# The second product of the attention scores over 128 rows instead of 64

## The chip, the cores and the metric

The kernel runs on one core of a Trainium2 chip. Its time is the device time of one execution in microseconds (us). The kernel before was timed three times: 2665.77, 2670.35 and 2674.51 us, median 2670.35 us. All arithmetic that the program sees is 32 bit; matrix products run on TensorE (PE), elementwise work on VectorE (DVE), ScalarE (ACT) and GpSimd (POOL), and most transfers are issued from SyncE's queue (SP).

## The reference, cut to what matters

The reference is one step of a four-layer decoder trunk of width 1024, for 512 tokens of a prompt and 8 single tokens of a sample group. Layer 1 mixes the tokens by dilated window attention, in three groups of 16 heads of 64 channels. The three groups have dilations 1, 4 and 16, and their outputs are merged by their softmax denominators. For the prompt, each group does this:

```
logits = einsum('brnqhd,brnkhd->brnhqk', qb, kb) * (Dh ** -0.5) + bias
logits = where(valid, logits, -1e30)
p = exp(logits - max(logits));  s = sum(p)
o = einsum('brnhqk,brnkhd->brnqhd', p, vb) / s;  lse = max + log(s)
```

The scores of one head thus contract over 64 channels. Before them stands `qkv = h @ w_qkv` (1024 by 9216), behind them `y @ w_o`.

## The kernel before, in words

Every 32-bit value that goes into a product is split into a rounded part hi and a rest lo (`copy` into a tile of the rounded type, then `tensor_sub`), and a product is the sum of hi by hi, lo by hi and hi by lo. `mm3` (lines 390 to 395) does this for the large products: three matmuls of 128 rows, on weights `wh`, `wh`, `wl` and moving operands `mh`, `ml`, `mh`. Tokens come in two chunks, CA (264 columns) and CB (256 columns).

The attention (`attn`, line 659) goes over eight pairs of heads. While pair `hp` is attended to (`attend`), the products of queries, keys and values of pair `hp + 1` (`qkv`) are put between its steps; behind the last pair it is the output's product (`attn_out`). A planner gives each engine one fixed order of instructions from this program and gives each tile a place in SBUF; a tile that takes the place of an earlier one waits for the last reader there. SyncE's queue works in order, so a transfer that waits for its place holds up those behind it.

For each pair and group, `qkv` leaves two tiles of 128 rows for the scores. In `qs`, a head's 64 rows of hi and its 64 rows of lo stand one above the other; in `ks` the keys' hi stands twice. One matmul over 128 rows gives hi by hi and lo by hi (line 927). The third part, hi of the queries by lo of the keys, is a second matmul over 64 rows: `qs[own]` with `kl[own]`, where `kl` is `[128, 512]`, with head 0 in rows 0 to 63 and head 1 in rows 64 to 127 (line 928). `kl` has three places in rotation.

`attn_units` makes the scores of two blocks of 128 queries: these matmuls, and then, for each block, a DVE pass that adds the bias and finds the minimum (L932) and an ACT exponential (L933). It is called eight times for a pair of heads: `scores_g0` four times and `scores_g12` four times. The biases come from DRAM by SyncE's queue (L939, L953), into a tile with three places. Later steps take the weights of the merge (`attn_weights`, POOL copies at L971 and L972), scale the exponentials (L1012, ACT), turn them (L1018, PE), split them (L1022, L1023) and multiply them by the values (L1038 to L1040). The exponentials lie in the place of `x`, which rests in DRAM meanwhile (`self.pr`); the outputs go to `y`.

The sample group's attention (`attn_sample`) goes along in steps: a transposed tile `st` that is sent to DRAM and read back spread out as `qt`, cache tiles `skv`, products on POOL (L1081, L1111) and sums on DVE (L1086, L1115) into a tile `part`.

The ring `w` of five places (`self.tp`, tag `w`) is used by the norms at a sublayer's start and end, and not in the middle of the attention. POOL has the additions `x + t` (L239) and some of the norms' sums (L222, L333) at the attention's start.

Of the kernel before, what the change touches and what calls it, by code (L numbers as in the profile page):

```python
# [36 lines left out]
# By the sublayer (0 to 7), and where a chunk is named by that too: which engine takes a share, and what goes first.  # L37
# [16 lines left out]
class Net:  # L54
# [19 lines left out]
    @contextmanager  # L74
    def phase(self, extra=0, start=0):
        """Working memory of a sublayer; extra: more tiles for weights beside the four that all share."""
        with ExitStack() as e:
            P = lambda name: e.enter_context(self.tc.tile_pool(name=self.n(name), bufs=1))
            lp = self.lp = P("lp")
            self.wx, self.wextra, self.wcount = (P("wx") if extra else None), extra, start  # L80
            yield lp
            self.wx = None
# [11 lines left out]
    # ---------------------------------------------------------------- set-up  # L94
# [17 lines left out]
    def load(self):  # L112
        """The tokens and the vectors by channel; the tokens are staged where the hidden units of chunk B will lie."""
# [33 lines left out]
    def load_tokens(self, t):  # L147
        """Block t of the tokens, channels on partitions."""
# [9 lines left out]
    def stir(self, n):  # L158
        """Products that nobody reads: TensorE's clock rises only while it works."""
        ps = self.psum(128, 128)  # L160
        for _ in range(n):
            self.nc.tensor.matmul(ps, self.ones, self.ones, start=True, stop=True)
# [4 lines left out]
    # ---------------------------------------------------------------- norms  # L167
    def rstat(self, acc, c, dim=D, eps=None):
        """acc [128, w]: per-partition sums of squares; returns 1/sqrt(sum/dim + eps) on all partitions (PSUM)."""
# [20 lines left out]
    def mean(self, acc, c):  # L190
        """The sum over the channels, on all partitions (PSUM)."""
# [5 lines left out]
    def post(self, gain):  # L197
        """The norm at a sublayer's end; gain(b): its factors (by channel) for block b of the output."""
        return {"gain": gain, "at": self.at}

    def post_block(self, post, ps, b, c, part=None, bias=None, scale=1.0, near_end=False):
        """One finished block of a sublayer's output: kept in y, its squares summed."""
# [21 lines left out]
    def post_end(self, post, c, next_row):  # L224
        """x += y * gain * r for chunk c, then the next sublayer's moving operand: by blocks; chunk B's is deferred."""
# [27 lines left out]
    def flush(self):  # L253
        """What the sublayer before left to be put behind the first products of this one."""
        self.run(self.deferred)

    def in_products(self, ww, c, rr, evac, fill=None):
        """Four products of chunk c, which evac(pg) takes up; at a sublayer's start the norms' work goes between."""
# [30 lines left out]
    def step_hooks(self):  # L289
        """Side work goes on a little: generators that load first and compute some steps later."""  # L290
# [4 lines left out]
    def out_order(self, goes_on=False):  # L295
        """The order of the last products' pairs of blocks: chunk A whole, then chunk B, and there first those
        whose weights' places the next sublayer's weights take."""
# [3 lines left out]
    def out_step(self, post, i, next_row):  # L301
        """After the i-th of the last products."""
# [19 lines left out]
    def pre_sums(self, c, at):  # L322
        """Per-partition sums of x's squares for the next norm, chunk c."""
# [11 lines left out]
    def pre_r(self, c):  # L335
        """1/rms of x for chunk c, in SBUF on all partitions."""
# [6 lines left out]
    # ---------------------------------------------------------------- weights  # L343
# [3 lines left out]
    def weights(self, ap, wide=False):  # L347
        """ap: up to 1024 rows by 128 columns in DRAM (wide: 128 rows by up to 1024 columns);
        returns the parts hi, lo as [128, blocks, 128]."""
# [19 lines left out]
    def behind(self, instructions):  # L369
        """What is traced within is issued after these, each on its own engine."""  # L370
# [5 lines left out]
    def ffn_in_weights(self, layer, jp):  # L376
        """Of the feed-forward's jp-th pair of hidden blocks: gate and up of each; perhaps loaded ahead."""
# [4 lines left out]
    def load_ahead(self, n):  # L382
        """The next n weights of the feed-forward that follows."""
# [13 lines left out]
    # ---------------------------------------------------------------- feed-forward  # L397
    def place(self, c, dtype):
        """Room for a third of chunk c's hidden units, in parts hi and lo; other sublayers use it in between."""
# [63 lines left out]
    # ---------------------------------------------------------------- pooling mixer  # L463
    def pool_bands_load(self):
        """What a token takes from the tokens before it, a band for each window, and from the sample group's history."""
# [3 lines left out]
    def pool(self, layer, j, post_row, next_row, begin=None):  # L469
        """The windows' means less the token are products of the normed tokens with bands of constants."""  # L470
# [49 lines left out]
    def pool_history(self, j):  # L520
        """What the windows take from the sample group's earlier inputs."""
# [13 lines left out]
    def pool_tokens(self, st, c):  # L535
        """The two blocks of tokens of chunk c, normed (but for the gain by channel), tokens on partitions."""
# [32 lines left out]
        if c == CB:  # L569
            # the last tokens, with the gains, are the prompt's new state  # L570
# [6 lines left out]
    def pool_sample(self, st):  # L577
        """The sample group's tokens: channels on partitions all along."""
# [22 lines left out]
    def pool_means(self, st, c, ahead=()):  # L601
        """Means less the token for chunk c: the moving operand of the pooling's product."""
# [25 lines left out]
    def pool_products(self, st, c, ahead=()):  # L628
        """ahead: the blocks before which a weight of the feed-forward is prepared."""
# [28 lines left out]
    # ---------------------------------------------------------------- attention mixer  # L658
    def attn(self, post_row, next_row):
# [4 lines left out]
        with self.phase() as self.ws:  # L664
            self.r = {}
            self.scr = [self.dram.tile([72, 128], F32, name=f"scr{i}") for i in range(8)]
            # x rests in DRAM meanwhile; its place holds the exponentials, y's the outputs
# [3 lines left out]
            self.wnext = None  # L671
            heads = [dict() for _ in range(9)]
# [18 lines left out]
    def attn_out(self):  # L691
        """The output's product of the first seven pairs of heads, as far as it hides behind the last pair."""
# [20 lines left out]
    def attn_out_end(self, post_row, next_row):  # L713
        """The rest: the last pair of heads, and the products that are left to hide the norm of chunk A."""
# [24 lines left out]
    def bias_setup(self):  # L739
        nc, I = self.nc, self.I  # L740
        # relative biases (negated, and 1e30 outside the window) as one row per head
# [31 lines left out]
        # the rows laid out for every query of a block, so that a head's biases load as one tile  # L773
# [16 lines left out]
    def qkv_weights(self, i):  # L790
        """Weights of the i-th product: for each pair of heads, queries and keys of each group, then values."""
# [4 lines left out]
    def qkv(self, hp, out):  # L796
        """Queries, keys (feature-major) and values (token-major) of a pair of heads, in parts hi and lo."""
# [7 lines left out]
        for gqs in ([(0, 1, 2)] if hp == 0 else []) + [(gq,) for gq in range(0 if hp else 3, 9)]:  # L805
# [21 lines left out]
            for gq, t in zip(gqs, ts):  # L827
                g, q = QKV_ORDER[gq]
                # of each head: the queries' parts hi and lo, one above the other, and for both the keys' part hi
# [6 lines left out]
                elif q == 1:  # L836
                    ks = ws.tile([128, 2, SEQ], F32R, tag="ks", name=self.n("ks"), bufs=3)
                    kl = ws.tile([128, SEQ], F32R, tag="kl", name=self.n("kl"), bufs=3)
                    for h, own, oth in HALVES:
                        nc.scalar.copy(ks[own, h], t[own])  # L840
                        nc.scalar.copy(ks[oth, h], t[own])
                        nc.vector.tensor_sub(kl[own], t[own], ks[own, h].bitcast(F32))
# [4 lines left out]
    def qkv_part(self, what, c, ps, t, sq9):  # L847
        """A finished product of chunk c, scaled, in the order of the group's residue classes."""
# [21 lines left out]
    def token_major(self, hp, g, q, t, out):  # L870
        """Keys and values with the tokens on partitions, for the caches and as the values' weights."""
# [19 lines left out]
    def attend(self, hp, kv):  # L891
        """Attention of a pair of heads; yields where other products can be put between."""
# [26 lines left out]
    def attn_units(self, h, units, bias, stat, lay, p):  # L919
        """Scores of two blocks of queries of head h: units = [(block, first key column, products)]."""  # L920
        nc, ws = self.nc, self.ws
        own = HALVES[h][1]
# [544 lines left out]
```

## Time and profile before

| what | value |
|---|---|
| median of three runs | 2670.35 us |
| the profiled execution's span, first to last instruction | 2664.7 us |
| PE busy / weight loads busy | 95% / 92% of the span |
| DVE / ACT / POOL busy | 66% / 50% / 19% |
| mean granted TensorE clock | 0.974 |
| the attention, from the first product to the last pair's end | about 455 to 1130 us |

The profiled execution has no time of its own beside its span; the span is 5.65 us below the median of the runs. A busy PE is not a PE at its peak: a matmul's record lasts from its start until its result has left, and the next one starts before that. So the distance from the start of one matmul to the start of the next tells what it costs. Weight loads have rows of their own (PEld).

### The profile page before, as it was taken

How to read it: one execution, taken by the hardware profiler on the slowest of the kernel's cores; microseconds unless marked ns; L12 is line 12 of the kernel's file. 1: busy time of each engine (PE TensorE's matmuls, PEld its weight loads, DVE VectorE, ACT ScalarE, POOL GpSimd, SP SyncE). 2: the span in 40 equal slices, each digit the busy share in tenths (PEclk: the TensorE clock that was granted, in tenths of full speed). 3: DMA queues.
4: the chain of work that ended last, by engine and by line, in shares of the span. 5: the costliest groups of instructions: out<-in, count | busy, mean ns of one | idle time of the engine just before them, and what ended most of it. 6: DMA issues, size and time to landing. Idle time of an engine off the chain costs nothing.

```text
span 2664.7 us, 50514 instructions
## 1 busy us (share of the span) xinstructions
PE 2539.0 (95%) x20200; PEld 2459.1 (92%) x20200; DVE 1762.4 (66%) x3063; ACT 1329.1 (50%) x2484; POOL 502.0 (19%) x661
## 2 busy tenths in 40 slices
PE   7999999999999999989999997679999998999998
PEld 7899999999999999889999985569999998999998
DVE  5746565677777777577474589987647456756564
ACT  6534344556655556455342373466534246644342
POOL 3100003123233322320000047622000004200002
PEclk8999999999999999999999998789999999999999
DMA  4575553444443443356464430023746452555451
GB/s 142 164 215 167 150 151 107 139 126 120 128 131 114 134 137 114 115 152 178 143 184 121 124 96 1 16 82 93 203 142 183 119 151 65 143 166 175 143 158 57
DMA packets 653432, 349.76 MB, mean 131 GB/s; under 512 B 14865, under 2 KB 649730, under 8 KB 652910
## 3 DMA queue, kind: packets, MB, share of 16 engines
q1 hardware_dynamic: 648996, 338.10, 43.9%
q0 software_dynamic: 1232, 6.06, 0.8%
q8 instruction: 159, 2.61, 0.4%
q10 hardware_dynamic: 2969, 2.37, 0.4%
q14 instruction: 76, 0.61, 0.1%
HBM read 331.87 MB, written 20.68 MB: 132 GB/s over the span
## 4 chain that ended last, share of the span: by engine, by line
PE 41%; DVE 7%; ACT 1%; POOL 1%; issue 1%; DMA 0%; DVEq 0%; ACTq 0%; POOLq 0%; SPq 0%
PE mm L393 13%; PE mm L394 13%; PE mm L395 13%; DVE y L1269 4%; DVE wl L365 1%; POOL acc L222 0%; PE mm L186 0%; POOL x L239 0%; ACT wh L364 0%; DVE y L1267 0%; DVE y L1274 0%; DVE ml L319 0%; DMA raw<-in_w_ffn_in_dram 0%; PE mm L615 0%; ACT mh L318 0%
## 5 line engine op out<-in xcount | busy, mean ns | idle before, releaser
L393 PE MATMUL mm<-mh,wh 128*128 128x264 f32 (+1 forms) x4544 | 1316.5, 291 | 34.2 <-DVE u L1179 19.9
L394 PE MATMUL mm<-ml,wh 128*128 128x264 f32 (+1 forms) x4544 | 1295.0, 285 | 5.6 <-DVE ml L319 5.4
L395 PE MATMUL mm<-mh,wl 128*128 128x264 f32 (+1 forms) x4544 | 1290.5, 284 | 0.7 <-DVE wl L365 0.7
L393 PEld LDWEIGHTS mm<-mh,wh 128*128 128x128 f32 x4544 | 865.0, 191 | 47.5 <-DVE u L1179 21.8
L364 ACT CAST wh<-raw 128x1024 fp32r<-128x1024 f32 (+1 forms) x557 | 574.0, 1036 | 661.8 <-PE mm L394 406.1
L394 PEld LDWEIGHTS mm<-ml,wh 128*128 128x128 f32 x4544 | 867.8, 191 | 11.5 <-DVE ml L319 8.7
L365 DVE TENSOR_TENSOR wl<-raw,wh 128x1024 fp32r<-128x1024 f32 (+1 forms) x557 | 691.8, 1246 | 279.9 <-ACT wh L364 277.0
L395 PEld LDWEIGHTS mm<-mh,wl 128*128 128x128 f32 x4544 | 865.8, 191 | 1.2 <-DVE wl L365 1.1
L393 PE MATMUL mm<-h,wh 128*128 128x264 f32 (+1 forms) x1408 | 398.5, 283 | 1.6 <-DVE pr L1154 1.6
L394 PE MATMUL mm<-h,wh 128*128 128x264 f32 (+1 forms) x1408 | 397.6, 282 | 0.8 <-DVE h L422 0.8
L395 PE MATMUL mm<-h,wl 128*128 128x264 f32 (+1 forms) x1408 | 397.9, 283 | 0.0
L222 POOL TENSOR_TENSOR acc<-acc,sq 128x264 f32<-128x264 f32 (+1 forms) x90 | 78.5, 872 | 1387.4 <-ACT sq L221 1384.1
L393 PEld LDWEIGHTS mm<-h,wh 128*128 128x128 f32 x1408 | 265.2, 188 | 2.6 <-issue 2.2
L394 PEld LDWEIGHTS mm<-h,wh 128*128 128x128 f32 x1408 | 265.2, 188 | 1.2 <-DVE h L422 1.0
L395 PEld LDWEIGHTS mm<-h,wl 128*128 128x128 f32 x1408 | 265.1, 188 | 0.1
L1269 DVE SCALAR_TENSOR_TENSOR y<-conv_u,vec,y 128x512 f32<-128x512 f32 (+1 forms) x136 | 131.4, 1001 | 0.0
L419 DVE TENSOR_TENSOR u<-mm,r 128x264 f32<-128x264 f32 (+1 forms) x176 | 74.8, 425 | 84.9 <-PE mm L395 84.8
L239 POOL TENSOR_TENSOR x<-x,xt 128x264 f32<-128x264 f32 (+1 forms) x111 | 97.7, 904 | 93.0 <-DVE xt L234 91.4
L1263 POOL TENSOR_TENSOR tapa<-tapa,tapp 128x512 f32<-128x512 f32 (+1 forms) x76 | 104.8, 1379 | 18.3 <-DVE y L1274 12.5
L456 DVE TENSOR_TENSOR y<-mm,y 128x264 f32<-128x264 f32 x64 | 24.0, 429 | 124.5 <-PE mm L395 124.5
L933 ACT ACTIVATE x<-x,own 128x256 f32<-128x256 f32 (+1 forms) x128 | 62.4, 489 | 87.8 <-DVE own L932 87.7
L417 DVE TENSOR_TENSOR g<-mm,r 128x264 f32<-128x264 f32 (+1 forms) x176 | 74.8, 425 | 42.5 <-PE mm L395 38.9
(221 smaller groups left out, 2704.0 us busy)
## 6 DMA issues: line engine op xcount, KB each, us to landing
raw<-in_w_ffn_in_dram SPq DMA_DIRECT2D x352, 512.0 KB
raw<-in_w_qkv_dram SPq DMA_DIRECT2D x72, 512.0 KB
raw<-in_w_ffn_out_dram SPq DMA_DIRECT2D x64, 512.0 KB
skv<-in_cache_swa_g_dram SPq DMA_DIRECT2D x32, 512.0 KB
raw<-in_w_ffn_out_dram SPq DMA_DIRECT2D x32, 384.0 KB
out_dram<-tm SPq DMA_DIRECT2D x32, 256.0 KB
raw<-in_conv_w_in_dram SPq DMA_DIRECT2D x16, 512.0 KB
bias<-bias_full SPq DMA_DIRECT2D x32, 128.0 KB
```

Source lines behind the costliest of these rows:

```text
L222: (eng or nc.vector).tensor_add(post[c], post[c], sq)
L239: self.added = nc.gpsimd.tensor_add(xb, xb, t)
L364: whi = nc.scalar.copy(wh, raw)
L365: self.parted = whi, nc.vector.tensor_sub(wl, raw, wh.bitcast(F32))
L393: nc.tensor.matmul(ps, wh[:, k, :], mh, start=first, stop=False)
L394: nc.tensor.matmul(ps, wh[:, k, :], ml, start=False, stop=False)
L395: nc.tensor.matmul(ps, wl[:, k, :], mh, start=False, stop=last)
L417: nc.vector.tensor_mul(g, pg[2 * i], rr[c])
L419: nc.vector.tensor_mul(u, pg[2 * i + 1], rr[c])
L933: nc.scalar.activation(pc, pc, AF.Exp, scale=-1.0, bias=stat[:, lay, 0, c:c + 1], accum_out=stat[:, lay, 1, c:c + 1])
L1263: nc.gpsimd.tensor_add(a2, ap, pr)
L1269: nc.vector.scalar_tensor_tensor(yb, win(ub, t), wd[:, b, t:t + 1], yb, op0=ALU.mult, op1=ALU.add)
```

## The change

`kl` becomes `[128, 2, 512]`, one half for each head. Head `h` has its own 64 rows of lo in `kl[own, h]`; the other 64 rows of that half are zero. The three tiles are made once, at the attention's start, and POOL sets their zero halves. The second matmul then takes all 128 rows: the queries' rows of lo meet the zeros. To make room, small tiles go elsewhere: the biases and `st` into the ring `w`, `qt` into the part of `y` that the last pair of heads will fill, and two of the three blocks of `part` into columns of `self.pr` that no block of queries uses. Comments and docstrings are gone.

```diff
             self.pending, self.late = [], []
             self.wnext = None
+            self.kl = [self.ws.tile([128, 2, SEQ], F32R, name=f"kl{i}") for i in range(3)]
+            for kl in self.kl:
+                for h, own, oth in HALVES:
+                    nc.gpsimd.memset(kl[oth, h].bitcast(F32), 0.0)
...
-                    kl = ws.tile([128, SEQ], F32R, tag="kl", name=self.n("kl"), bufs=3)
+                    kl = self.kl[(hp * 3 + g) % 3]
                     for h, own, oth in HALVES:
                         nc.scalar.copy(ks[own, h], t[own])
                         nc.scalar.copy(ks[oth, h], t[own])
-                        nc.vector.tensor_sub(kl[own], t[own], ks[own, h].bitcast(F32))
+                        nc.vector.tensor_sub(kl[own, h], t[own], ks[own, h].bitcast(F32))
...
-        own = HALVES[h][1]
...
                 nc.tensor.matmul(out, qs[:, h, qc], ks[:, h, kc], start=True, stop=False)
-                nc.tensor.matmul(out, qs[own, h, qc], kl[own, kc], start=False, stop=True)
+                nc.tensor.matmul(out, qs[:, h, qc], kl[:, h, kc], start=False, stop=True)
...
-            bias = ws.tile([128, 256], F32, tag="bias", name=self.n("bias"), bufs=3)
+            bias = self.tp.tile([128, 264], F32, tag="w", name=self.n("bias"), bufs=5)[:, :256]
...
-        st = ws.tile([72, 128], F32, tag="st72", name=self.n("st72"), bufs=1)
+        st = self.tp.tile([128, 264], F32, tag="w", name=self.n("st72"), bufs=5)[:72, :128]
...
-        qt = ws.tile([128, 3, 128], F32, tag="sqt", name=self.n("sqt"), bufs=1)
+        qt = self.y[:, 7, NS:NS + 384].rearrange("p (g f) -> p g f", g=3)
...
-        part = ws.tile([128, 3, 128], F32, tag="spart", name=self.n("spart"), bufs=1)
+        part = [ws.tile([128, 128], F32, tag="spart", name=self.n("spart"), bufs=1)] + [self.pr[0][h][:, 0, 0:128] for h in range(2)]
```

## Rows read from the trace of the kernel before

**Rows 1.** Busy time by stretch: us, then PE, PEld, DVE, ACT, POOL, clock, DMA.
```profile
674.00:701.00 27.00, 27.00 (x170) 22.88 (x168) 18.26 (x48) 14.58 (x40) 15.21 (x27) 1.00 0.38 110
701.00:748.00 47.00, 47.00 (x418) 46.82 (x419) 36.20 (x66) 28.19 (x56) 8.02 (x14) 1.00 0.46 133
...
1065.00:1091.00 26.00, 26.00 (x150) 21.67 (x149) 10.08 (x32) 11.39 (x37) 12.67 (x27) 0.95 0.33 94
```

**Rows 2.** Groups by line, 460 to 1130 us: count, busy us, mean ns, idle before.
```profile
L928 PE MATMUL mm<-kl,qs 64*128 64x128 f32 x192 | 65.0, 339 | 0.0
```

**Rows 3.** PE in order of time, a call of `scores_g12`: start, duration, what.
```profile
687.96 0.22 PE L927 MATMUL mm<-ks,qs 128*128 128x128 f32 x1
688.11 0.33 PE L928 MATMUL mm<-kl,qs 64*128 64x128 f32 x1
688.37 0.33 PE L927 MATMUL mm<-ks,qs 128*128 128x128 f32 x1
...
689.90 0.39 PE L393 MATMUL mm<-mh,wh 128*128 128x256 f32 x1
690.12 0.28 PE L394 MATMUL mm<-ml,wh 128*128 128x256 f32 x1
```

**Rows 4.** PE, first and last rows of two calls of `scores_g0`.
```profile
674.27 0.22 PE L927 MATMUL mm<-ks,qs 128*128 128x128 f32 x1
...
675.53 0.28 PE L394 MATMUL mm<-ml,wh 128*128 128x264 f32 x1
...
676.87 0.27 PE L927 MATMUL mm<-ks,qs 128*128 128x256 f32 x1
...
678.23 0.28 PE L394 MATMUL mm<-ml,wh 128*128 128x256 f32 x1
```

**Rows 5.** Matmuls and weight loads in order of time, around a first score product.
```profile
673.19 0.28 PE L393 MATMUL mm<-mh,wh 128*128 128x264 f32 x1
673.19 0.19 PEld L394 LDWEIGHTS mm<-ml,wh 128*128 128x128 f32 x1
673.31 0.29 PE L394 MATMUL mm<-ml,wh 128*128 128x264 f32 x1
...
674.42 0.18 PEld L928 LDWEIGHTS mm<-kl,qs 64*128 64x128 f32 x1
674.43 0.32 PE L928 MATMUL mm<-kl,qs 64*128 64x128 f32 x1
```

**Rows 6.** PE, matmuls of 128 columns elsewhere in the attention.
```profile
640.65 0.22 PE L1038 MATMUL mm<-th,vh 128*64 128x128 f32 x1
640.71 0.22 PE L1039 MATMUL mm<-tl,vh 128*64 128x128 f32 x1
...
643.61 0.60 PE L1018 MATMUL mm<-ident,x 128*128 128x128 f32 x4
643.97 0.37 PE L393 MATMUL mm<-mh,wh 128*128 128x256 f32 x1
```

**Rows 7.** DVE, ACT and PE behind the last scores of a pair.
```profile
701.18 0.42 DVE L932 CUSTOM_DVE_ANT_0 x<-mm,bias 128x256 f32<-128x256 f32 x1 [1.16 <-PE mm L928]
...
707.42 4.00 ACT L1012 ACTIVATE x<-x,ca 128x256 f32<-128x256 f32 x10
...
711.33 0.60 PE L1018 MATMUL mm<-ident,x 128*128 128x128 f32 x4
```

**Rows 8.** POOL: a memset (group by line), and its order around the attention's start.
```profile
L1165 POOL MEMSET conv_u<- 128x240 f32 x1 | 0.3, 288 | 0.0
...
456.80 2.14 POOL L239 TENSOR_TENSOR x<-x,xt 128x264 f32<-128x264 f32 x3
...
462.61 0.75 POOL L333 TENSOR_TENSOR acc<-acc,sq 128x264 f32<-128x264 f32 x1 [1.88 <-DVE acc L333]
```

**Rows 9.** Waits of SyncE's queue, 500 to 1100 us: total us, times, longest.
```profile
SPq L953 <- DVE own L932: 43.0, 10, 6.3
SPq L354 <- DVE own L932: 35.9, 7, 5.3
```

More of the change, by code (lines that the diff above doesn't have):

```diff
@@ L951, in scores_g12 @@
         for h in range(2):
-            bias = ws.tile([128, 256], F32, tag="bias", name=self.n("bias"), bufs=3)
+            bias = self.tp.tile([128, 264], F32, tag="w", name=self.n("bias"), bufs=5)[:, :256]
             nc.sync.dma_start(bias, self.bias_full[2 * hp + h, :, 256:512])
@@ L1114, in attn_sample @@
         for (g, o, n), vt in zip(SLOTS, vts):
-            nc.vector.tensor_reduce(part[:, g, :], vt.rearrange("p s f -> p f s"), axis=AX.X, op=ALU.add)
-        nc.vector.tensor_add(part[:, 0, :], part[:, 0, :], part[:, 1, :])
-        nc.vector.tensor_add(part[:, 0, :], part[:, 0, :], part[:, 2, :])
+            nc.vector.tensor_reduce(part[g], vt.rearrange("p s f -> p f s"), axis=AX.X, op=ALU.add)
+        nc.vector.tensor_add(part[0], part[0], part[1])
+        nc.vector.tensor_add(part[0], part[0], part[2])
         ps = self.pstat(128, 16)
-        nc.tensor.matmul(ps[:, 0:8], part[:, 0, :], self.sel, start=True, stop=True)
+        nc.tensor.matmul(ps[:, 0:8], part[0], self.sel, start=True, stop=True)
         for h in range(2):
```

## The prediction, made before the changed kernel was run

> **What bounds the kernel now.** I read the page's share of busy time first (PE 95%), then the busy time by stretch of the attention, since only there does the change touch anything. The two stretches from 674 to 748 us are one pair of heads, 74 us: PE is busy for all 74 and its clock is full, while DVE has 18.26 + 36.20 = 54.46, ACT 42.77 and POOL 23.23 [rows 1]. So PE sets the pace, and time taken off its queue is time off the kernel, as long as no other engine comes late. Next I read the groups by line for the products concerned: 192 second score products over 64 rows [rows 2], 24 for each of 8 pairs of heads, with 192 first ones beside them. Their mean duration tells little, since records overlap. What counts is the distance between starts, so the third view is PE in order of time.
>
> There the scores stand out. In the large products 264 columns start every 0.12 us (673.19 to 673.31) [rows 5]. In a call of `scores_g12`, products of only 128 columns start 0.15 us (first to second) and 0.26 us (second to third) apart, and so on to the eighth. The large product behind them starts its successor late too: from the first score product to that successor, 687.96 to 690.12, it is 2.16 us [rows 3]. The reason is in the weight loads. Between products of 128 rows the load of the next starts together with the product before it (both at 673.19), and so is hidden. The load for the 64-row product starts at 674.42, 0.15 us after the first score product's start at 674.27 [rows 4], and its own product follows at 674.43 [rows 5]: PE runs empty between. The way back to 128 rows costs as much: of the pair of starts 0.26 us apart in rows 3, the second is a 128-row product. I take it that going from 128 rows to 64 and back is what costs, not the size of either.
>
> **The change part by part.** *The products.* Nothing is added or removed in number: 384 score matmuls before and after. What changes is the distance between starts. For 256 columns over 128 rows I take 0.12 us, from the 264 columns [rows 5]. For 128 columns on 128 columns of weights, in the scores' number type and without a change of rows, the trace has no row. Below it lies 0.06 us, the distance of the values' products, with 128 columns but only 64 columns of weights [rows 6]; above it 0.12 us, that of twice the columns. The nearest row is the transposes, 128 columns on 128 columns of weights: four last 0.60 us in all, the last about 0.27 of that, so three distances make 0.33 us, 0.11 each [rows 6]. I take 0.109.
>
> A pair of heads makes eight calls. Four are of `scores_g12`, with eight products of 128 columns: 2.16 us until the second large matmul [rows 3], and after the change 8 x 0.109 + 0.12 = 0.99, which saves 1.17. Two are of the first kind in `scores_g0`, with two products of 128 and two of 256 columns: 674.27 to 675.53 is 1.26 us [rows 4], after it 2 x 0.109 + 3 x 0.12 = 0.58, which saves 0.68. Two are of the second kind, four products of 256 columns: 676.87 to 678.23 is 1.36 us [rows 4], after it 0.60, which saves 0.76. Together 4 x 1.17 + 2 x 0.68 + 2 x 0.76 = 7.56 us for a pair, 60.5 us for eight. With 0.06 it would be 74.6 us, with 0.12 it would be 57.3.
>
> The Trainium skill (TensorE: Matmul & The Clock Gate, Back-to-back issue gap) gives some 81 ns for a stream of loads and products at 128 columns, where the transposes here show 109. By it 36 products of a pair would each be 0.028 us shorter and the sum 68.6 us. The same page (Part 3, The mechanism) says that a weight load overlaps a running product only when it goes to another group of rows. That would speak against the change, since two products of 128 rows share all their rows. The trace disagrees: 128-row loads start with the product before, and it is the 64-row load that does not.
>
> *What comes late next.* The scores of a pair lie within 27 us (674 to 701), where DVE works for 18.26 [rows 1]. With 7.56 us less, DVE has 19.4 us for the same work, in order, and some of its waits there are for ACT and POOL, not for PE. Today it waits for PE at the last scores (1.16 us before 701.18) [rows 7]. After the change I expect it to finish them some 2 us behind PE. What hangs on them are the merge's weights, the scaling and the transposes. The scaling of the first two blocks is done at about 707.42 + 2 x 0.4 = 708.2, and PE turns them at 711.33 [rows 7], a slack of 3.1 us. So this chain bears a lag of 2 us; weights being split in the same stretch, behind it in DVE's queue, have less room. Bounds for what is given back in a pair: nothing (the slack takes it all), and 7.56 us (DVE cannot be compressed at all). I take 1 us for each of seven pairs, near the lower end, because DVE still has room in the rest of the 74 us of a pair. In the last pair DVE works only 10.08 of 26 us [rows 1]; there I take nothing. Given back: 7 us.
>
> *The zeros.* Six memsets on POOL, 64 rows by 512. The nearest row has 240 elements in 0.288 us [rows 8]; by elements that makes 0.61 us each, 3.7 in all. If the place still belongs to the feed-forward's last products, they come late and stand in POOL's queue among the additions to `x` (456.80), which PE waits for, and the norm's sums. POOL idles 1.88 us before 462.61 [rows 8], which hides half. Bounds 0 and 3.7 us; I take 0.5, since additions ahead of that gap come earlier in the program.
>
> *The moved tiles.* Biases and `st` make five tiles a pair in a ring of five, so each waits for a reader one pair back, where three places made SP's queue wait for L932 (43.0 us in ten waits, and 35.9 at weight transfers behind them) [rows 9]. PE did not wait for any of that, so its going gains nothing; the cover is the weights' lead of several us, and a wait beyond it would cost one for one. `qt` and `part` change place only: same instructions, sizes and order of readers. The three places of `kl` rotate as before. I cost these at 0, with a bound of 2 us either way for another order in SP's queue.
>
> *Sum.* 60.5 - 7 - 0.5 = 53.0 us less. The span goes from 2664.7 to 2611.7; the median of the runs is 5.65 us above the span, and with the same distance the time is 2617.4 us.
>
> **The rivals.** *More than that.* Short products could start every 0.06 us, and the slack could take DVE's lag: 2670.35 - 74.6 = 2595.8, or 2609.9 with 0.109 and nothing given back. For it: the values' products do 0.06. Against it: they load half the columns.
>
> *DVE becomes the bound in the scores.* Of the 7.56 us of a pair it gives back half, 3.8, in eight pairs 30 us: 2640. For it: 18.26 us of DVE's work would fill 94% of the shorter stretch. Against it: PE has products of the next pair to go on with, and DVE has slack behind the scores.
>
> *It does not do what it says.* The distance could come from something other than the rows, such as loads that two score products in a row cannot hide. Then the 128-row products stand 0.15 to 0.26 us apart as now and only the memsets remain: 2670 to 2674. The Trainium skill's rule on row groups, above, would lead here. Against it: large products hide the same load, and the transposes of 128 columns start every 0.11 us.
>
> *Slower.* A bias's transfer that waits for a place in the shared ring heads SP's queue, with the next weights behind it. The planner may put it ahead of readers of the same pair, so that it waits through the scores, up to 20 us. It decides from where it exceeds the weights' lead by what the change saves. Nine weights in 74 us are 8.2 us each; two raw tiles ahead make 16.4, of which I allow 5 for landing and splitting, so the lead is about 11 us (an estimate). PE then stands still 20 - 11 = 9 us in each of eight pairs, 72 us: 2617 + 72 = 2689. For it: SP did wait for L932 with three places. Against it: the longest of these waits was 6.3 us [rows 9], and places go from three to five.
>
> **How the numbers follow.** Forecast 0.66 (2606 to 2630), more than that 0.10, DVE half 0.15, no change 0.05, slower 0.04. The range from 2600 to 2642 takes in the DVE case and the lower half of the first rival and leaves out 0.18. A measurement of this kernel tells 0.3%, some 8 us, from no change. Faster by more holds the first three cases, 0.91; no change 0.05; slower 0.04.
>
> **What will show it.** In PE's order of time the second score product should read 128*128 and start 0.11 us behind the first, its load with the product before, and a call of `scores_g12` should last about 1.0 us until the second large matmul. The eight calls' sum should be near 7.6 us less in a pair, and a pair should take some 66 us where it takes 74. What is given back should show as PE idle with DVE as releaser behind the scores, under 1.5 us a pair. In POOL's order the memsets should not stand ahead of the additions to `x`. The prediction is wrong if products of 128 rows still stand 0.2 us apart, if PE waits for DVE several us a pair, or if weight transfers wait behind biases.

## The result, and the profile after

The changed kernel takes 2635.7 us, the median of four runs (2632.74 to 2639.77), against 2672.43 for the kernel before on the same chip (four runs, 2665.77 to 2677.61): a ratio of 0.9858, 95% interval 0.9837 to 0.988. It is faster by 36.7 us. The forecast was 2617.4 within 2600 to 2642: the sign is right and the time lies in the range, but a third of the expected 53 us is missing. The case that had the largest chance, 2606 to 2630, did not come about; 2635.7 lies nearer to the rival in which DVE becomes the bound (2640).

From the profile's page after: the span, then busy time, share of the span and number of instructions by engine.

```profile
span 2638.0 us, 50548 instructions
...
PE 2490.6 (94%) x20200; PEld 2437.6 (92%) x20200; DVE 1764.8 (67%) x3063; ACT 1326.9 (50%) x2484; POOL 503.1 (19%) x667
```

PE has as many instructions as before, POOL six more: the memsets. Next, PE in order of time in a call of `scores_g12` (start, duration, line, shape), which answers to [rows 3], and matmuls and weight loads at the start of another call, which answer to [rows 5].

```profile
685.28 0.22 PE L931 MATMUL mm<-ks,qs 128*128 128x128 f32 x1
685.34 0.28 PE L932 MATMUL mm<-kl,qs 128*128 128x128 f32 x1
685.45 0.28 PE L931 MATMUL mm<-ks,qs 128*128 128x128 f32 x1
...
686.12 0.34 PE L393 MATMUL mm<-mh,wh 128*128 128x264 f32 x1
686.29 0.29 PE L394 MATMUL mm<-ml,wh 128*128 128x264 f32 x1
```
```profile
682.27 0.23 PE L931 MATMUL mm<-ks,qs 128*128 128x128 f32 x1
682.27 0.19 PEld L932 LDWEIGHTS mm<-kl,qs 128*128 128x128 f32 x1
682.33 0.28 PE L932 MATMUL mm<-kl,qs 128*128 128x128 f32 x1
```

The products stand 0.11 us apart where they stood 0.26 (the first two of a call 0.06, where they stood 0.15), the load of the second product starts together with the first product, and the call lasts 1.01 us (685.28 to 686.29) where it lasted 2.16. Summed over all 64 calls, from the first score product to the second large matmul, it is 51.8 us instead of 112.2: 60.4 us less, where 60.5 was forecast.

Now what PE waited for between 500 and 1100 us (total us, times, longest): before, then after.

```profile
PE mm L878 <- DVE srd L1123: 4.4, 1, 4.4
```
```profile
PE mm L1043 <- DVE tl L1027: 6.5, 10, 1.6
PE mm L883 <- DVE t L873: 5.9, 7, 0.9
PE mm L883 <- DVE srd L1128: 4.4, 1, 4.4
PE mm L1022 <- ACT x L1016: 2.7, 5, 0.9
PE mm L1097 <- DVE smp L1094: 2.1, 1, 2.1
...
```

The first view has one row in all, which after still stands there unchanged (the reciprocals in the last pair). The rows for `t` (DVE's part of the next pair's products), for the scaling (`x`) and for `smp` are new. Of the row for `tl` (the splits of the turned exponentials) three waits, 2.0 us, are the last pair's: the kernel before has the same three behind 1100 us, outside this window. The other seven, 4.5 us, are new.

How long a pair of heads takes is read from the first score product of pair 0 and of pair 6, six pairs later: before, then after.

```profile
520.76 0.22 PE L927 MATMUL mm<-ks,qs 128*128 128x128 f32 x1
...
982.41 0.22 PE L927 MATMUL mm<-ks,qs 128*128 128x128 f32 x1
```
```profile
527.72 0.22 PE L931 MATMUL mm<-ks,qs 128*128 128x128 f32 x1
...
961.26 0.22 PE L931 MATMUL mm<-ks,qs 128*128 128x128 f32 x1
```

(982.41 - 520.76) / 6 = 76.94 us before, 72.26 after: 4.7 us less in a pair, of 7.55 that the products save. From the end of PE's last score product of a pair to the end of DVE's last pass over scores it was 0.81 us; after the change it is 3.3 to 4.6 us, by pair, and 0.81 in the last. This distance is called DVE's lag below.

The 26.7 us between the two spans come from five parts, cut at the same PE instructions in both. From the attention's start (in the middle of the first feed-forward's products) to the first score: 81.34 to 85.06, +3.7. Pairs 0 to 6: 545.77 to 512.44, -33.3. The last pair: 130.65 to 125.16, -5.5. These make -35.1, close to the medians' 36.7. What lies ahead (+3.2 us) and behind (+5.1) runs the same instructions in the same order in both kernels; over the profiles of all kernels here these stretches take 439.4 to 444.3 and 1465.4 to 1475.3 us, so both lie within what differs from run to run.

### The profile page after: what moved, and what is told of

It is laid out like the page before. It is cut to its first block, busy times and chain, and to the rows that moved or that the text cites. A ratio compares the mean times of both kernels' runs of the same rounds, so it can differ in the third digit from the quotient of the medians.

```text
span 2638.0 us, 50548 instructions
## 1 busy us (share of the span) xinstructions
PE 2490.6 (94%) x20200; PEld 2437.6 (92%) x20200; DVE 1764.8 (67%) x3063; ACT 1326.9 (50%) x2484; POOL 503.1 (19%) x667
## 5 line engine op out<-in xcount | busy, mean ns | idle before, releaser
L365 DVE TENSOR_TENSOR wl<-raw,wh 128x1024 fp32r<-128x1024 f32 (+1 forms) x557 | 691.9, 1246 | 284.1 <-ACT wh L364 281.8
L394 PEld LDWEIGHTS mm<-ml,wh 128*128 128x128 f32 x4544 | 868.0, 191 | 12.4 <-DVE ml L319 10.1
```

The costliest lines, as they stand in the source:

```text
L365: self.parted = whi, nc.vector.tensor_sub(wl, raw, wh.bitcast(F32))
L394: nc.tensor.matmul(ps, wh[:, k, :], ml, start=False, stop=False)
```

## The experiments

Two questions were open. Is it really the change between 128 and 64 rows that cost time? And why is 2.9 us of each pair given back, and 3.7 us at the start? The theory for the second: POOL multiplies the cached keys of the sample's attention by the queries (L1085, before L1081) within the scores, and DVE instructions beside it take longer; DVE, with less time for the scores, then finishes late. Rivals: DVE simply has too much work there; the place of that product is wrong, since the moved tiles shifted it; or any lag behind the scores counts, whatever its source. Every kernel is compared with the kernel before on its own chip.

**The rows by themselves (e1).** The kernel before, but in a call all 128-row products go first and then all 64-row ones, so that the number of rows changes twice in a call instead of at every product. In this order part of the scores' sums is lost; the instructions and their sizes are the same.

```diff
-                nc.tensor.matmul(out, qs[:, h, qc], ks[:, h, kc], start=True, stop=False)
-                nc.tensor.matmul(out, qs[own, h, qc], kl[own, kc], start=False, stop=True)
+                nc.tensor.matmul(out, qs[:, h, qc], ks[:, h, kc], start=True, stop=False, skip_group_check=True)
+        for i, (col, skip, parts) in enumerate(units):
+            for qs, (ks, kl), qc, kc, o, n in parts:
+                out = s[:, i, o:o + n]
+                nc.tensor.matmul(out, qs[own, h, qc], kl[own, kc], start=False, stop=True, skip_group_check=True)
```

> The kernel before, with the score products of a call in another order: first all products over 128 rows, then all over 64. Theory (a change from 128 rows to 64, or back, is what costs; 1.15 us for eight such changes in a call of scores_g12, 0.14 each): only two changes are left in a call, so such a call lasts 1.0 + 0.29 = 1.3 us until the second large matmul (2.16 before, 1.01 after the change), a 64-row load starts with the 64-row product before it, a pair of heads saves some 4.9 us of PE, and the time is 2640 to 2650. Rival (a 64-row product costs 0.25 us whatever stands before it): 4 x 0.11 + 4 x 0.25 + 0.12 = 1.56 us or more a call, 2655 to 2665. Rival (loads of short products cannot be hidden at all): 2.1 us, 2672.

Measured: 2632.55 us, ratio 0.9857 [0.9838, 0.9877], below the 2640 to 2650 that were expected. PE in order of time, one call:

```profile
677.71 0.56 PE L927 MATMUL mm<-ks,qs 128*128 128x128 f32 x4
678.20 0.66 PE L931 MATMUL mm<-kl,qs 64*128 64x128 f32 x4
678.79 0.39 PE L393 MATMUL mm<-mh,wh 128*128 128x256 f32 x1
679.02 0.28 PE L394 MATMUL mm<-ml,wh 128*128 128x256 f32 x1
```

677.71 to 679.02 is 1.30 us. The single starts are 0.06, 0.11, 0.11 | 0.21 | 0.16, 0.11, 0.11 | 0.20 apart: 0.11 between 64-row products as between 128-row ones, and more only where the rows change. Six changes fewer save 2.16 - 1.30 = 0.86, or 0.14 us a change; the two that are left are the 0.29 us to the 1.01 of the changed kernel. The number of rows costs nothing, a change of it does. (The Trainium skill, "TensorEngine Tiling (Array Packing)", Key Properties, says that a change of tiling mode drains TensorE. The 0.14 us a change fit that; the drain itself no row shows.) And something else shows: this kernel saves only 38.3 us in its score calls, not 60.4, and is as fast as the changed one. Its pairs take (954.21 - 521.50) / 6 = 72.12 us, all of its 4.8 us a pair are kept, and DVE's lag is 0.9 to 1.2 us: here the scores of a pair last 22.0 us and not 19.5, and DVE still gets through them in time.

**The zeros (e2).** The memsets are moved behind the last addition to `x`.

```diff
-            for kl in self.kl:
-                for h, own, oth in HALVES:
-                    nc.gpsimd.memset(kl[oth, h].bitcast(F32), 0.0)
...
+                if begin and lo > 0:
+                    with self.behind((self.added,)):
+                        for kl in self.kl:
+                            for h, own, oth in HALVES:
+                                nc.gpsimd.memset(kl[oth, h].bitcast(F32), 0.0)
```

> The changed kernel, with the six memsets put behind the last addition to x on POOL. Theory (the memsets among the additions cost 3 to 4 us at the attention's start): from the last feed-forward product to the first score product it takes 3 to 4 us less than in the changed kernel, 68 instead of 71 to 72 us; the time is 2632. Rival (the start differs for another reason, such as the moved biases): no difference at the start, 2635.7.

Measured: 2634.78 us, 0.9858 [0.9835, 0.9881]. POOL in order of time, the changed kernel and then this one (idle before a row and its releaser in brackets):

```profile
461.55 0.52 POOL L676 MEMSET kl<- 64x512 f32 x1
462.15 1.05 POOL L239 TENSOR_TENSOR x<-x,xt 128x264 f32<-128x264 f32 x1
...
466.06 2.22 POOL L676 MEMSET kl<- 64x512 f32 x4
468.29 0.74 POOL L333 TENSOR_TENSOR acc<-acc,sq 128x264 f32<-128x264 f32 x1
```
```profile
474.29 1.77 POOL L239 TENSOR_TENSOR x<-x,xt 128x256 f32<-128x256 f32 x2 [0.76 <-DVE xt L234]
476.12 3.37 POOL L831 MEMSET kl<- 64x512 f32 x6
```

In the changed kernel they stood among the additions and sums that PE waits for. Moved, the stretch up to the first score takes 82.6 us instead of 85.1. Over all kernels with the memsets among the additions it takes 85.0 and 85.1, without them there 80.9 to 82.6. So they cost 2.5 to 4 us. In the total this cannot be told apart.

**The moved tiles (e4).** The kernel before with 64 rows, and only the small tiles at their new places.

```diff
-            bias = ws.tile([128, 256], F32, tag="bias", name=self.n("bias"), bufs=3)
+            bias = self.tp.tile([128, 264], F32, tag="w", name=self.n("bias"), bufs=5)[:, :256]
...
```

> The kernel before, with the moved tiles alone: biases and st in the ring w, qt in y, part in the exponentials' place; the second product stays over 64 rows, and kl as it was. Theory (the moves cost nothing that PE sees): 2672 +- 4, a pair of heads takes 77.0 us as before; POOL's product of the cached keys starts 2 to 3 us later within a pair, since four biases stand ahead of its transfers in SP's queue. Rival (the moves are part of what is given back): a pair takes 78 us or more, 2680.

Measured: 2673.56 us, 0.9999 [0.9982, 1.0016]; a pair takes (986.68 - 525.03) / 6 = 76.94 us, as before. The moves do shift the product of the cached keys, from 8.9 to 13.2 us into a pair, but on its own that costs nothing.

**Without the product of the keys (e3), and its control (e8).** The changed kernel and the kernel before, each without that product on POOL (the sample's scores are then sums of the cached keys).

```diff
-            nc.gpsimd.tensor_mul(kt, kt, qt[:, g:g + 1, :].to_broadcast([128, n, 128]))
```

> The changed kernel without POOL's product of the cached keys by the queries (three instructions a pair; the sample group's scores are then sums of keys). Theory (the PE time given back, some 2.9 us a pair, comes from DVE finishing the scores 4.2 us behind PE, because POOL's product stretches DVE's instructions beside it and holds up the copies of the merge): DVE ends 1 to 2.5 us behind PE, PE's waits before the transposes vanish, and a pair takes 69.5 to 70.5 us instead of 72.3; time 2615 to 2625. Rival (DVE's own 20 us of work in the 19.5 us of the scores are the bound): the lag stays over 3.5 us and a pair takes 71.5 us or more; 2630 to 2636.

> The kernel before without POOL's product of the cached keys (the sample group's scores are then sums of keys). Control for e3. Theory (in the kernel before the stretched DVE instructions are hidden, the slack before the transposes being 3.0 us): a pair takes 77.0 us as before, time 2668 to 2674, and the slack grows by under 1 us. Rival (the product costs PE time there too): under 76 us a pair, 2660.

Measured: 2614.34 us, 0.9786 [0.9754, 0.9818], for the changed kernel without it, and 2674.6 us, 1.0007 [0.9995, 1.0019], for the kernel before. How the product acts is seen in DVE's and POOL's order within the scores of one pair, in the changed kernel:

```profile
686.45 3.43 DVE L365 TENSOR_TENSOR wl<-raw,wh 128x1024 fp32r<-128x1024 f32 x1 [0.54 <-ACT wh L364]
...
690.49 2.67 DVE L847 TENSOR_TENSOR kl<-t,ks 64x512 fp32r<-64x512 f32 x2
...
694.83 0.41 DVE L936 CUSTOM_DVE_ANT_0 x<-mm,bias 128x256 f32<-128x256 f32 x1
...
697.92 0.17 DVE L979 TENSOR_TENSOR cm<-own,oth 128x16 f32<-128x16 f32 x1 [2.67 <-POOL oth L976]
...
708.09 1.39 DVE L847 TENSOR_TENSOR kl<-t,ks 64x512 fp32r<-64x512 f32 x2
```
```profile
683.47 5.33 POOL L1085 TENSOR_TENSOR skv<-skv,y 128x1152 f32<-128x1152 f32 x2
...
690.69 1.92 POOL L1085 TENSOR_TENSOR skv<-skv,y 128x640 f32<-128x640 f32 x1
```

PE's last score product ends at 690.71 + 0.27 = 690.98, and DVE's last pass over scores at 694.83 + 0.41 = 695.24, a lag of 4.3 us. The weights' split (L365), 3.43 us beside POOL's product, takes 1.22 alone (at 679.91); the keys' split (L847) takes 2.67 for two, alone 1.39 (the row at 708.09). That is 2.21 + 1.28 = 3.5 us, as much as the lag grew (0.8 to 4.3 us). DVE's busy time from the first score product of this pair to the end of the last pass (the number that (x52) follows), before, after and in e3:

```profile
674.27:701.96 27.69, 27.69 (x175) 23.50 (x174) 18.77 (x52) 14.70 (x39) 15.21 (x27) 1.00 0.37 105
```
```profile
671.51:695.26 23.75, 23.75 (x205) 23.71 (x204) 19.92 (x52) 14.55 (x39) 14.14 (x24) 1.00 0.47 129
```
```profile
663.71:684.00 20.29, 20.29 (x176) 20.25 (x175) 16.47 (x52) 14.53 (x39) 5.71 (x21) 1.00 0.54 150
```

DVE's 52 instructions take 16.5 us without the product and 19.9 with it. The same place without the product, the last pass and the step behind it:

```profile
683.57 0.42 DVE L936 CUSTOM_DVE_ANT_0 x<-mm,bias 128x256 f32<-128x256 f32 x1
...
686.64 0.18 DVE L979 TENSOR_TENSOR cm<-own,oth 128x16 f32<-128x16 f32 x1 [2.65 <-POOL oth L976]
```

The wait of that step for POOL's copies of the merge's weights is the same with the product (2.67 us) and without (2.65), so it is DVE that comes late and not those copies. Without the product the lag is 0.8 to 1.3 us, a pair takes (941.72 - 525.23) / 6 = 69.42 us, and all of the 7.5 us is kept. In the kernel before the product is hidden: without it a pair still takes 76.94. There, too, a split beside it took 3.20 us, but DVE had time to catch up:

```profile
683.70 3.20 DVE L365 TENSOR_TENSOR wl<-raw,wh 128x1024 fp32r<-128x1024 f32 x1 [0.34 <-ACT wh L364]
...
695.13 1.40 DVE L842 TENSOR_TENSOR kl<-t,ks 64x512 fp32r<-64x512 f32 x2
```
```profile
683.16 2.66 POOL L1081 TENSOR_TENSOR skv<-skv,sqt 128x1152 f32<-128x1152 f32 x1
```

The product is needed, so the next six runs look for a place for it, or for slack to bear it. All have the memsets of e2.

**More of PE's work behind the scores (e5).** Six steps of the next pair's products instead of four go between the scores and the transposes.

```diff
-ATT_STEPS, FILL_STEPS = 31, 72
+ATT_STEPS, FILL_STEPS = 33, 72
...
-        for _ in range(4):
+        for _ in range(6):
             yield
```

> The changed kernel with the memsets late (as in e2) and with more of the next pair's products between the last scores and the transposes: six steps there instead of four, the fill spread over 33 steps instead of 31. Theory (PE has too little to do while DVE, 4.2 us behind, and the merge's weights come in): some 3.1 us of PE's work moves into that gap, the waits before the transposes go, and a pair takes 69.4 to 70.2 us instead of 72.3; time 2612 to 2622. Rival (the waits only move to what DVE does next, t and tl): a pair takes 71.5 us or more, 2632.

Measured: 2656.96 us, 0.9944 [0.9925, 0.9964], 75.45 us a pair: a miss. What PE waited for:

```profile
PE mm L885 <- DVE t L875: 19.6, 7, 3.2
PE mm L1045 <- DVE tl L1029: 7.9, 7, 1.1
```

The wait for the scaling is gone, but PE now comes to the next products' results before DVE has taken them up: 2.8 us a pair where it was 0.8. Work that is put ahead of one wait is missing ahead of the next.

**The product earlier in the scores (e6).** The cached keys are loaded before the second two biases, and the product follows at 7.3 to 9.1 us into a pair, about as early as in the kernel before (8.9).

```diff
+        next(smp)
...
-            kt = cache_tile(g, 0, n)
+            kts.append(cache_tile(g, 0, n))
+        yield
+        for (g, o, n), kt in zip(SLOTS, kts):
             nc.gpsimd.tensor_mul(kt, kt, qt[:, g:g + 1, :].to_broadcast([128, n, 128]))
-            kts.append(kt)
```

> The changed kernel with the memsets late, and with the loads of the cached keys traced ahead of the second two biases of a pair, so that they come earlier in SP's queue. Theory (POOL's product stretches those DVE instructions that end the scores, and the moved biases have put it there): it starts at 10 us of a pair instead of 12.0, DVE ends the scores 2.5 to 3.5 us behind PE instead of 4.2, and a pair takes 71 to 71.8 us; 2627 to 2632. Rival (its place does not matter, only its amount): 72.3 us and 2634.

Measured: 2639.55 us, 0.9876 [0.9853, 0.99], 72.72 us a pair, DVE 3.1 to 5.7 us behind: a miss. The keys' splits are free of the product in pairs 1 to 6, but other splits lie beside it now. In pair 5 it is the queries' split, two of which take 1.39 us in the changed kernel:

```profile
898.20 5.79 DVE L841 SCALAR_TENSOR_TENSOR qs<-t,qs 64x512 fp32r<-64x512 f32 x2
```
```profile
896.84 6.61 POOL L1090 TENSOR_TENSOR skv<-skv,y 128x1152 f32<-128x1152 f32 x2 [18.95 <-DVE t L875]
```

That is 4.4 us more, and this pair has the longest lag. An earlier place within the scores changes which split stands beside the product, and DVE has no time left there to catch up.

**The product on DVE (e7).** It stays in the scores, but POOL has only the small copies of the merge there.

```diff
-            nc.gpsimd.tensor_mul(kt, kt, qt[:, g:g + 1, :].to_broadcast([128, n, 128]))
+            nc.vector.tensor_mul(kt, kt, qt[:, g:g + 1, :].to_broadcast([128, n, 128]))
```

> The changed kernel with the memsets late and POOL's product of the cached keys made by DVE instead. Theory (sharing, not the amount of DVE's work, is what loses): DVE has some 3.3 us more of its own work and no stretched instructions; it ends the scores 1 to 2.5 us behind PE and a pair takes 70 to 71.5 us. Rival (DVE's amount of work counts): its product falls in the crowded time behind the scores, and a pair takes 72.3 us or more.

Measured: 2620.83 us, 0.9807 [0.979, 0.9824], 70.87 us a pair, DVE 2.2 to 3.5 us behind. No split is stretched: L365 takes 1.22 us again, two of the keys' 1.40. But the product is DVE's own work now, and up to the end of its last pass DVE is busy for 19.6 to 19.8 us in pairs 1 to 6, much as in the changed kernel (19.3 to 20.2). So the lag is shorter, but partly above the 1 to 2.5 us that were expected: DVE's amount of work counts in the scores as well. Of the waits, those for the scaling are gone; 2.8 us in four for `t` and 6.6 in ten for `tl` (2.0 in three of the last pair's) are left.

**Copies on ACT (e9 with the product on DVE, e10 with it on POOL).** DVE's copies of the outputs to `y` go to ACT, to take load off DVE behind the scores.

```diff
-            nc.vector.tensor_copy(self.y[fs, hp, NS:TOK].rearrange("p (b j r) -> p b r j", b=4, r=4),
+            nc.scalar.copy(self.y[fs, hp, NS:TOK].rearrange("p (b j r) -> p b r j", b=4, r=4),
```

> As e7 (memsets late, the product of the cached keys on DVE), and the copies of a head's finished output to y on ACT instead of DVE, two of 1.07 us a pair. Theory (DVE's lag behind the scores is what PE waits for, and one of these copies stands at the head of the scores on DVE): DVE ends the scores 1 us sooner than in e7, the waits before the transposes go, those for t and tl shrink, and a pair takes 69.5 to 70.3 us instead of 70.9; time 2610 to 2618. Rival (what is left of the waits is set behind the scores, by DVE's order there): 70.9 us and 2621.

> The changed kernel with the memsets late and the copies to y on ACT; the product of the cached keys stays on POOL. Theory (any microsecond taken from DVE before or in the scores shortens its lag one for one): DVE ends the scores some 3.2 us behind PE instead of 4.2, and a pair takes 70.5 to 71.5 us instead of 72.3. Rival (only the sharing with POOL counts): 72.3 us.

Measured: 2627.57 us, 0.9825 [0.9803, 0.9846], and 2642.95 us, 0.9883 [0.9866, 0.9899]; 71.92 and 73.79 us a pair. Both are misses: in each a pair takes longer than in its counterpart with the copies on DVE (70.87 us in e7, 72.49 in e2), though the intervals of the times overlap. In e10 the lag grew to 3.3 to 7.3 us and PE waited 13.0 us in seven waits for the scaling. The traces show a wait that grew with it. DVE's passes over the scores wait for the biases, 11.6 us in ten waits in e9 and 14.4 in ten in e10, where it was 3.3 in four (e7) and 2.7 in four (e2). In pair 3 of e10, which has the longest lag, DVE and ACT show:

```profile
750.75 0.29 DVE L938 CUSTOM_DVE_ANT_0 x<-mm,bias 128x128 f32<-128x128 f32 x1 [3.51 <-DMA bias<-bias_full]
```
```profile
741.05 1.09 ACT L1049 COPY y<-mm 64x512 f32<-64x512 f32 x1
742.17 0.26 ACT L1059 COPY st<-mm 72x128 f32<-72x128 f32 x1
```

The copy to `y` now stands on ACT ahead of the copy to `st`, and SP's queue, in which the second bias comes behind the transfers of `st`, waits for that copy: 10.0 us in six waits (e9) and 10.1 in six (e10), against 3.2 in seven (e7) and 2.5 in six (e2). This wait is shorter than the delay of the biases, and no run takes it away by itself: it is part of the cause at most, and the rest stays open.

**The product on DVE, behind the merge's weights (e11).** DVE does it, but only after everything that hangs on the scores.

```diff
-            nc.gpsimd.tensor_mul(kt, kt, qt[:, g:g + 1, :].to_broadcast([128, n, 128]))
+            with self.behind((self.weighed,)):
+                nc.vector.tensor_mul(kt, kt, qt[:, g:g + 1, :].to_broadcast([128, n, 128]))
```

> As e7, but DVE makes the product of the cached keys only behind the merge's weights. Theory (DVE's work in the scores sets the lag, what comes behind them sets the waits for t and tl): DVE ends the scores 0.8 to 1.3 us behind PE, no wait before the transposes, but 3.5 us more of DVE's work stands before t and tl, so these waits grow, and a pair takes 70.9 to 73 us. Rival (only the lag behind the scores counts): 69.4 us, as without the product.

Measured: 2617.16 us (2604.03 to 2620.67), 0.9776 [0.9751, 0.9801], the lowest median of those that compute everything. Its interval lies apart from the changed kernel's, but overlaps with e7's [0.979, 0.9824]. DVE behind the scores, and the first score products of pairs 0 and 6:

```profile
682.38 0.18 DVE L981 TENSOR_TENSOR cm<-own,oth 128x16 f32<-128x16 f32 x1 [2.63 <-POOL oth L978]
684.34 3.36 DVE L1088 TENSOR_TENSOR skv<-skv,y 128x1152 f32<-128x1152 f32 x3
```
```profile
520.73 0.22 PE L933 MATMUL mm<-ks,qs 128*128 128x128 f32 x1
...
938.32 0.22 PE L933 MATMUL mm<-ks,qs 128*128 128x128 f32 x1
```

A pair takes 69.60 us (in the profiled run, the fastest of the four), 7.3 less than before; DVE is 0.8 to 1.2 us behind, and the transposes have 2.0 to 2.4 us of slack (3.0 before). The three products take 3.36 us together on DVE, after the step that starts the merge's weights. The rival that only the lag at the scores' end counts is right: DVE's total work is the same as in e7. The product behind the merge's weights but still on POOL was not tried.

## Why the prediction was right, and where it was not

**The products: right, mechanism and size.** 60.4 us against 60.5, and 0.11 us against 0.109. That the sum fits so closely is in part luck: the first distance of a call is 0.06 us and not 0.109, the large product behind the scores starts 0.17 us after the last of them, and the two nearly cancel. That the change of rows costs, and not their number, was chosen from [rows 3 to 5]; e1 shows it by itself. The rival by which two products that share all their rows cannot hide a load is refuted twice: 128-row loads start with the product before, and in e1 64-row products stand 0.11 us apart as well.

**What comes late next: right mechanism, size wrong.** This is the step that failed. It gave back 1 us a pair, 7 in all; measured is 52.9 - 33.3 = 19.6 us for pairs 0 to 6, 2.8 us a pair. It expected DVE 2 us behind and a slack of 3.1 us before the transposes. In the pair shown DVE was 4.3 us behind; the transposes, which came 3.0 us after the scaling of their two blocks, now start 0.35 us before the second block is done, so the slack is used up. The working took DVE's busy 18.26 us [rows 1] as work that stays the same. It does not: 2.0 us of it were already one split standing beside POOL's product (3.20 us against 1.22), and after the change it is 3.5 us in two kinds of splits. DVE's own work in the scores is 16.5 us (e3). POOL's 15.21 us in the same row were read as another engine's load, and not as something that lengthens DVE's rows. e3, e7 and e11 show it, and e8 shows that it had been hidden. The forecast's own rival, DVE as the bound, named the size (half of the 7.56 us) but not this cause, and e3 shows that DVE gets through its work in the shorter time when POOL's product is gone. Each pair of the first seven now has three pauses, read from PE's starts (usually 0.12 us apart): 0.4 to 1.2 us at the transposes, about 1.1 at `t` and 0.9 at `tl`, together some 17 of the 19.6 us. The last two lie in DVE's queue behind the late work, of which the prediction had named only the weights' splits, without a price.

**The last pair: nothing given back was expected, 2.0 us it was** (7.55 - 5.5). This is not established: the kernels with 64-row products in their old order take 130.65, 134.20 (e4) and 132.77 us (e8) for the last pair, at a granted clock of 0.93 to 0.94, and the changed kernel 125.16 at 0.96. DVE is not late there (0.81 us); the new wait is one for the sample's sums (L1097, 2.1 us), and it is gone in e3, e7 and e11, where POOL does not make the product.

**The zeros: 0.5 us expected, 2.5 to 4 measured** (e2). The instruction was over-estimated (0.56 us each, against 0.61), but the additions that were hoped to come ahead of them did not.

**The moved tiles: 0, right** (e4). Of [rows 9], the biases' waits are gone in the changed kernel and the weights' transfers wait longer instead, 64.5 us against 35.9, yet PE waited for no weights. The slower rival, a bias ahead of the weights, did not come about.

**Slips in the sums.** A pair was put at 74 us, from the two stretches of [rows 1]; it takes 76.9, as the next pair's first score shows. And the distance from span to run was taken as 5.65 us, between the span of one execution and the median of three; the changed kernel's profiled run is 1.8 us (2639.77) above its span, and of the three runs before the nearest, 2665.77, is 1.1 us above. Neither touches the difference. The range, as it is described, leaves out 0.05 + 0.04 and half of 0.10, which is 0.14 and not 0.18.

With the measured sizes the sum is 60.4 - 19.6 - 2.0 - 3.7 = 35.1 us, against 36.7 [32 to 44 by the ratio's interval].

## What to carry to other kernels

When PE's work in a stretch shrinks, check the engine that must finish with it in that stretch row by row against the same instructions elsewhere: rows of DVE that are two to three times their usual length beside a POOL instruction are hidden only as long as there is slack, and the next speed-up may use it up. Here it paid to move such work to DVE and behind the chain that the next PE step waits for (e11); adding PE's work ahead of one wait made the next wait longer (e5). And a matmul with half of its operand zero cost no more here than one of half the rows (0.11 us both), while each change between the two cost 0.14 us, more than the product.

## What the runs showed of the hardware

A DVE instruction with two operands in SBUF stands still beside a POOL instruction of that kind, and does not merely slow down. In the changed kernel POOL's second product ends at 683.47 + 5.33 = 688.80 and the split beside it (L365) at 686.45 + 3.43 = 689.88, 1.08 us later; before, POOL ends at 685.82 and the split at 683.70 + 3.20 = 686.90, again 1.08 later, nearly its whole 1.22 us alone. In pairs 1 to 6 of the changed kernel this split begins at different times and takes 2.9 to 3.5 us, and it always ends 1.08 to 1.09 us behind the product. POOL waits in the same way: in pair 1 of e6 the split beside the first product ends at 607.71, 1.08 us behind it, and POOL's next product, begun at 606.59, takes 3.64 us where the first took 2.67. DVE's passes over the scores, with one operand in PSUM, keep their 0.41 us beside the product. The Trainium skill ("SBUF — State Buffer", Who interferes with whom) says that a DVE instruction with two inputs in SBUF contends with a GpSimd instruction that reads SBUF, because its second input comes through a read interface that the two share, and calls that an exclusive lock. These rows agree.

Six memsets of 64 x 512 take 3.37 us on POOL (e2). The first two score products of a call stand 0.06 us apart in the changed kernel and the others 0.11; why the first distance is shorter was not tried.
